# One store split into nine strided transfers, and fifteen tiny reads added, in an RMSNorm and matmul kernel

## The chip, the cores and the metric

The kernel runs on one core of one Trainium2 chip. The metric is the device time of one execution in microseconds (us). The kernel before took 210.04 us, the median of three runs (209.98 to 210.21).

## What is computed

The input x has 16,384 rows of 512 float32. Each row is divided by its root mean square and multiplied by gamma; the result goes through a matrix of 512 x 768:

```python
rms = np.sqrt(np.mean(x ** 2, axis=-1, keepdims=True) + eps)
x_norm = x / rms * gamma
return np.matmul(x_norm, weight).astype(np.float32)
```

## The kernel before

**Tiles.** The rows are worked in 128 tiles of 128 rows (`NT` = 128, `P` = 128), two tiles to a turn of the main loop (line 473, `NP` = 64 turns). A tile's row t of partition p is not row 128 t + p: sixteen tiles share a stretch of 2,048 rows in which each partition owns 16 rows that follow one another, so that a transfer moves long whole pieces per partition. The function `rows` (line 206) makes this view of x or of the output; for n tiles it gives an array of 128 partitions x n tiles x row.

**One tile.** x is loaded into `xt` (two buffers of sixteen tiles). GpSimd casts it to bf16 (`cast`, line 251); ScalarE sums the squares (`square`, line 258), and a root and a reciprocal give `rstd`. TensorE transposes pairs of bf16 as 32-bit words (line 292) and VectorE copies the transposed block out of PSUM (line 301); of some tiles VectorE does the transposition alone in blocks of 32 (lines 326 to 340). Then TensorE multiplies by the weights, which carry gamma (line 373), into one of three accumulators. ScalarE takes even tiles and VectorE odd tiles out of the accumulator, scaled by `rstd`, into `ot` (`finish_tile`, line 385).

**Transfers.** `ot` has three buffers of eight tiles, so the output goes out by eights: `o_first` and `o_size` (line 204) say which tiles make one store, and `store` (line 355) issues it when its last tile is done. The first eight tiles go as 1, 1, 2 and 4, tiles 112 to 119 as 4 and 4, the last eight as 4, 2 and 2. A new tile can be written into `ot` only when the store of 24 tiles before has landed. x comes in pieces of 2, 2, 4, 8, 8, 8, three of 16, and then pairs of 8 (line 203); `load_until` (line 247) issues them about 20 tiles ahead. All of these transfers are issued by SyncE, one after another in the order of the program, 39 in all: 22 stores, 15 loads of x and 2 of the weights. ScalarE issues one, for gamma: 2 rows of 1,024 B. So whatever is put ahead of a transfer on SyncE, a wait or an issue, holds back all those behind it.

**Order.** The class `Order` records every operation with what it reads and writes. Its method `emit` (line 37) works out the waits that are needed, gives each transfer a semaphore of its own (or one that is known to be done with) that counts to 16, and emits the streams; the middle turns of TensorE become a loop (line 152). Transfers that no later operation waits for are collected in `left` (line 163), and ScalarE waits for them at the end (line 506). The very last store (tiles 126 and 127) is issued behind everything else and is awaited last by SyncE (lines 508 to 512).

**Around the change.** The store of tiles 72 to 79 is issued in turn 39, behind the loads of tiles 96 to 111 and ahead of the store of tiles 80 to 87. The store of tiles 112 to 115 is issued in turn 57; behind it come those of 116 to 119, 120 to 123, 124 and 125, and 126 and 127, and no more loads. A store of four tiles is 128 rows of 12,288 B (1,536 KB), one for each partition.

Of the kernel before, what the change touches and what calls it, by code (L numbers as in the profile page):

```python
# [11 lines left out]
F32 = mybir.dt.float32  # L12
# [4 lines left out]
P = 128  # L17
# [149 lines left out]
def kernel(  # L167
# [9 lines left out]
    PE, DVE, ACT, POOL, SP = nc.tensor, nc.vector, nc.scalar, nc.gpsimd, nc.sync  # L177
    order = Order(tc)
# [4 lines left out]
    x = x.flatten_outer_dims()  # L183
    out = out.flatten_outer_dims()
# [3 lines left out]
    NT = N // P  # L188
    NP = NT // 2
    XG, OG = 16, 8  # L190
# [15 lines left out]
    def rows(ap, i, n):  # L206
        base, t = (x_first[i], x_size[i]) if i < XG else (i - i % XG, XG)
        return ap[base * P:(base + t) * P, :].rearrange("(p t) d -> p t d", t=t)[:, i - base:i - base + n, :]

    def sb(name, shape, dtype):  # L210
        return nc.alloc_sbuf_tensor(name, shape, dtype).ap()
# [13 lines left out]
    xTq = sb("xTq", [P, 4, 2, P, 2], BF16)  # L225
    ot = [sb(f"ot{n}", [P, OG, O], F32) for n in range(3)]
    told = sb("told", [P, 1], F32)
    ssq = sb("ssq", [P, NT], F32)
    rms = sb("rms", [P, NT], F32)
    rstd = sb("rstd", [P, NT], F32)  # L230
# [4 lines left out]
    def cells(name, slot, i, n=1):  # L235
        return [(name, slot, t) for t in range(i, i + n)]
# [118 lines left out]
    def store(i):  # L355
        first, n = o_first[i], o_size[i]
        s = first // OG % 3
        if i == first + n - 1:
            src = ot[s][:, first % OG:first % OG + n, :]
            order.transfer(SP, lambda: SP.dma_start(out=rows(out, first, n), in_=src), reads=cells("ot", s, first % OG, n))  # L360

    def hold(lhsT, cell):
        run(PE, lambda: PE.ldweights(lhsT), [cell])  # L363
# [21 lines left out]
    def finish_tile(i, engine):  # L385
        a = accumulator(i)
        s = i // OG % 3
        ends = i == o_first[i] + o_size[i] - 1 and i > o_first[i]
        before = [("told", i - 1)] if ends else []
        scale(engine, ot[s][:, i % OG, :], ops[a][:, :O], rstd[:, i:i + 1],  # L390
              [("ops", a, 0), ("ops", a, 1), ("rstd", i)] + before, [("ot", s, i % OG)])
        store(i)
        if engine is ACT and i + 1 == o_first[i] + o_size[i] - 1:
            run(ACT, lambda: ACT.mul(out=told, in_=eps_sb, mul=1.0), ["eps"], ["told", ("told", i)])  # L394
# [154 lines left out]
```

## Time and profile before

| What | Value |
|---|---|
| runs shown, median of 3 | 210.04 us |
| profiled execution, own time | 210.62 us |
| its span, first to last instruction | 208.8 us |
| granted TensorE clock, mean | 0.988 |
| TensorE busy | 194.5 us (93%) |
| VectorE, ScalarE, GpSimd busy | 149.4, 146.2, 59.8 us |
| bytes moved | 85.55 MB, HBM read 35.13, written 50.33 |
| chain that ended last, by engine | PE 71%, DMA 15%, DVE 6% |
| issue to landing, store of 8 tiles, median | 16.3 us |
| issue to landing, stores of tiles 112 to 115 and 116 to 119 | 12.0 and 9.4 us |
| issue to landing, last store, issued at 200.8 | 7.1 us |
| one store's issue on SyncE, median | 333 ns |
| one load's issue on SyncE, least, median, most | 340, 539, 823 ns |

The profile is of one execution. Its first part gives the busy time of each engine; the second cuts the span into 40 equal slices, in which a digit is the busy share in tenths. PE is TensorE's matrix multiply and PEld its weight load, DVE is VectorE, ACT ScalarE, POOL GpSimd, SP SyncE; a q behind a name means the queue of that engine, with its waits and issues. The DMA row is the mean busy share of the core's 16 DMA engines. The third part lists the DMA queues: q1 is the one that SyncE issues to, q10 ScalarE's, q8 and q14 fetch instructions. The trace behind the page has a record of each packet with its start, duration, size and queue, but not the engine that moved it.

### The profile page before, as it was taken

The page shows a single profiled execution, that of the slowest core. Times are in us where ns is not written, and L with a number is a line of the kernel's source. Part 1 is how long each engine was busy: PE and PEld are TensorE (multiplying, and loading weights), DVE is VectorE, ACT ScalarE, POOL GpSimd, SP SyncE. Part 2 cuts the span into 40 slices and gives each one's busy share as a digit, 9 for nine tenths or more (in the row PEclk, how much of TensorE's full clock was granted, in tenths as well). Part 3 has the DMA queues.
Part 4 walks back from the last instruction along what each step waited for, and adds up shares of the span by engine and source line. Part 5 has one row for each costly group of instructions (what it writes and reads, how often), then busy time and mean ns, then how long its engine had stood idle before and what let it go on. Part 6 is the DMA issues. An engine that isn't in the chain of part 4 may idle for free.

```text
span 208.8 us, 2821 instructions
## 1 busy us (share of the span) xinstructions
PE 194.5 (93%) x1236; PEld 72.7 (35%) x717; DVE 149.4 (72%) x255; ACT 146.2 (70%) x363; POOL 59.8 (29%) x34
## 2 busy tenths in 40 slices
PE   7789979999999999999999999999999999999910
PEld 1234433443344333342344333443333334433200
DVE  0455645999569975999469984999569984999410
ACT  4698888677877498774977787677877688673310
POOL 3147633009300093004900651006700265000000
PEclk9999999999999999999999999999999999999995
DMA  6999999999999999999999999999999999999991
GB/s 227 426 439 430 377 385 430 477 405 430 405 388 414 369 438 424 454 402 449 428 413 446 408 450 428 414 438 425 443 433 414 452 408 438 438 433 400 420 414 78
DMA packets 5628, 85.55 MB, mean 410 GB/s; under 512 B 626, under 2 KB 628, under 8 KB 1780
## 3 DMA queue, kind: packets, MB, share of 16 engines
q1 hardware_dynamic: 5616, 85.46, 97.4%
q8 instruction: 3, 0.05, 0.1%
q14 instruction: 5, 0.04, 0.0%
q10 hardware_dynamic: 4, 0.00, 0.0%
HBM read 35.13 MB, written 50.33 MB: 409 GB/s over the span
## 4 chain that ended last, share of the span: by engine, by line
PE 71%; DMA 15%; DVE 6%; issue 2%; SPq 1%; ACT 1%; POOL 1%; ACTq 0%
PE ps L367 62%; DMA xt<-in_x_dram 15%; PE ps L296 8%; DVE ot L350 2%; DVE xTq L340 2%; DVE xT L309 1%; POOL xb L254 1%; ACT jk L262 0%; SPq L416 0%; SPq L243 0%; ACT ot L348 0%; DVE xTq L309 0%; SPq L360 0%; DVE rstd L269 0%; SPq L544 0%
## 5 line engine op out<-in xcount | busy, mean ns | idle before, releaser
L367 PE MATMUL ps<-w_bf,xT 128*128 128x512 bf16 (+1 forms) x768 | 141.8, 326 | 1.4 <-DVE w_bf L350 0.9
L348 ACT ACTIVATE ot<-ps,rstd 128x768 f32<-128x768 f32 x64 | 57.4, 897 | 42.4 <-PE ps L367 41.2
L262 ACT ACTIVATE jk<-xt 128x512 bf16<-128x512 f32 x128 | 78.7, 618 | 6.9 <-DMA xt<-in_x_dram 6.9
L254 POOL CAST xb<-xt 128x2048 bf16<-128x2048 f32 (+3 forms) x21 | 46.2, 2218 | 114.5 <-DMA xt<-in_x_dram 95.7
L350 DVE TENSOR_SCALAR ot<-ps,rstd 128x768 f32<-128x768 f32 x64 | 64.8, 1013 | 9.0 <-PE ps L367 8.4
L363 PEld LDWEIGHTS <-xT 128*128 128x128 bf16 x384 | 37.7, 98 | 58.2 <-issue 56.9
L296 PE MATMUL ps<-ident_f,xb 128*128 128x128 f32 x200 | 54.2, 275 | 0.9 <-POOL xb L254 0.9
L340 DVE STREAM_TRANSPOSE xTq<-xq 32x256 f32<-32x256 f32 x112 | 48.8, 435 | 3.4
L367 PE MATMUL ps<-w_bf,xTq 128*128 128x512 bf16 (+1 forms) x256 | 49.0, 326 | 1.2 <-DVE xTq L309 1.2
L309 DVE COPY xT<-ps 128x1024 bf16<-128x1024 bf16 (+1 forms) x51 | 33.1, 652 | 23.1 <-PE ps L296 21.5
L296 PEld LDWEIGHTS ps<-ident_f,xb 128*128 128x128 f32 x200 | 28.4, 143 | 46.2 <-issue 42.9
L262 ACT ACTIVATION_READ_ACCUMULATOR jk<-xt 128x1 f32 x128 | 24.3, 190 | 0.0
L363 PEld LDWEIGHTS <-xTq 128*128 128x128 bf16 x128 | 12.5, 98 | 17.8 <-issue 16.1
L329 POOL CAST xq<-xt 128x2048 bf16<-128x2048 f32 x7 | 13.3, 1893 | 0.0
L269 DVE RECIPROCAL rstd<-rms 128x8 f32<-128x8 f32 (+3 forms) x20 | 3.9, 193 | 8.0 <-ACT rms L267 7.8
L267 ACT ACTIVATE rms<-ssq,eps_sb 128x8 f32<-128x8 f32 (+3 forms) x20 | 6.0, 300 | 0.6
L367 PE MATMUL ps<-warm 128*128 128x512 bf16 x10 | 4.4, 578 | 1.4 <-DVE eps_sb L425 1.4
L394 ACT ACTIVATE told<-eps_sb 128x1 f32<-128x1 f32 x20 | 3.8, 192 | 0.0
L309 DVE COPY xTq<-ps 128x1024 bf16<-128x1024 bf16 x2 | 1.4, 692 | 2.4 <-PE ps L296 2.4
L348 ACT ACTIVATE w_bf<-w_f,g_sb 128x768 bf16<-128x768 f32 x2 | 1.9, 935 | 1.5 <-DMA w_f<-in_weight_dram 0.9
L446 DVE COPY g_sb<-ps 128x4 f32<-128x4 f32 x1 | 0.2, 161 | 3.2 <-PE ps L440 3.2
L412 ACT ACT_TABLE_LOAD x1 | 1.3, 1283 | 1.5 <-SPq L503 1.5
(12 smaller groups left out, 3.6 us busy)
## 6 DMA issues: line engine op xcount, KB each, us to landing
out_dram<-ot SPq DMA_DIRECT2D x13, 3072.0 KB, 16.3
xt<-in_x_dram SPq DMA_DIRECT2D x9, 2048.0 KB, 21.0
xt<-in_x_dram SPq DMA_DIRECT2D x3, 4096.0 KB, 22.1
out_dram<-ot SPq DMA_DIRECT2D x4, 1536.0 KB, 12.0
out_dram<-ot SPq DMA_DIRECT2D x3, 768.0 KB, 8.2
w_f<-in_weight_dram SPq DMA_DIRECT2D x2, 768.0 KB, 5.7
xt<-in_x_dram SPq DMA_DIRECT2D x2, 512.0 KB, 5.2
xt<-in_x_dram SPq DMA_DIRECT2D x1, 1024.0 KB, 9.2
```

The source lines that it names most:

```text
L254: run(POOL, lambda: POOL.tensor_copy(out=xb[s][:, i % 8:i % 8 + n, :], in_=src), of, cells("xb", s, i % 8, n))
L262: run(ACT, lambda: ACT.activation(out=jk[j], in_=src[:, 0, :], func=AF.Square, accum_out=ssq[:, i:i + 1]), of, [("jk", j), ("ssq", i)])
L267: run(ACT, lambda: ACT.activation(out=rms[:, s], in_=ssq[:, s], func=AF.Sqrt, scale=1.0 / D, bias=eps_sb), [("ssq", t) for t in range(i, i ...
L269: run(DVE, lambda: DVE.reciprocal(out=rstd[:, s], in_=rms[:, s]), [("rms", i)], [("rstd", t) for t in range(i, i + n)])
L296: run(PE, lambda: PE.transpose(out=tp[b][:, t, h, :], in_=words[:, lo:lo + P], identity=ident_f), cells("xb", s, j % 4 * 2 + t) + ["ident" ...
L309: run(DVE, lambda: DVE.tensor_copy(out=dst[:, t:t + n, :], in_=src[:, t:t + n, :]), [("tp", b)], to[t:t + n])
L329: run(POOL, lambda: POOL.tensor_copy(out=xq[s], in_=src), of, [("xq", s)])
L340: run(DVE, lambda: DVE.transpose(out=dst, in_=src), [("xq", s)], ["xTq"])
L348: run(ACT, lambda: ACT.mul(out=dst, in_=src, mul=r), reads, writes)
L350: run(DVE, lambda: DVE.tensor_single_scalar(out=dst, in_=src, scalar=r, op=mybir.AluOpType.mult), reads, writes)
L363: run(PE, lambda: PE.ldweights(lhsT), [cell])
L367: run(PE, lambda: PE.add_instruction(mybir.InstMatmult(name=nc.get_next_instruction_name(), engine=mybir.EngineType.PE, ins=[PE.lower_ap(r ...
```

## The change

The store of tiles 112 to 115 (`first == NT - 16`) becomes nine transfers. Transfer `lo` takes the partitions lo, lo + 9, lo + 18 and so on: 15 partitions for lo = 0 and 1, 14 for the other seven, 128 together, with the same 12,288 B for each. Behind the store of tiles 72 to 79, SyncE issues fifteen reads of the first rows of x: read k takes k rows of 4k + 12 numbers (64 to 288 B a row, 120 rows in all) into new buffers `few` that nothing else reads or writes. The buffers take 2,640 B in each of 16 partitions.

```diff
     told = sb("told", [P, 1], F32)
+    few = {k: sb(f"few{k}", [16, 4 * k + 12], F32) for k in range(1, 16)}
     ssq = sb("ssq", [P, NT], F32)
...
         if i == first + n - 1:
             src = ot[s][:, first % OG:first % OG + n, :]
-            order.transfer(SP, lambda: SP.dma_start(out=rows(out, first, n), in_=src), reads=cells("ot", s, first % OG, n))
+            for lo in range(9) if first == NT - 16 else (None,):
+                part = slice(None) if lo is None else slice(lo, P, 9)
+                to, of = rows(out, first, n)[part], src[part]
+                order.transfer(SP, lambda to=to, of=of: SP.dma_start(out=to, in_=of), reads=cells("ot", s, first % OG, n))
+            if first == 72:
+                for k in range(1, 16):
+                    order.transfer(SP, lambda k=k: SP.dma_start(out=few[k][:k, :], in_=x[:k, :4 * k + 12]), writes=[("few", k)])
```

Each of the 23 additional transfers has a semaphore of its own and is one more that ScalarE waits for at the end. Nothing else differs.

## The prediction

> **What bounds the kernel now.** I read the page's slices first, then its queue rows, then the stretches at the end, then what SyncE waited for. All times are from the span's start. The page:
>
> ```profile
> span 208.8 us, 2821 instructions
> ...
> PE   7789979999999999999999999999999999999910
> ...
> DMA  6999999999999999999999999999999999999991
> ...
> DMA packets 5628, 85.55 MB, mean 410 GB/s; under 512 B 626, under 2 KB 628, under 8 KB 1780
> ...
> q1 hardware_dynamic: 5616, 85.46, 97.4%
> ...
> q10 hardware_dynamic: 4, 0.00, 0.0%
> ```
>
> TensorE and the transfers are both full, but TensorE stops one slice before the transfers do. Busy time by stretch (columns: length, PE, PEld, DVE, ACT, POOL with counts, granted clock, DMA share, GB/s):
>
> ```profile
> 189.00:195.00 6.00, 6.00 (x38) 1.86 (x19) 5.20 (x8) 1.89 (x3) 0.00 (x0) 1.00 1.00 425
> 195.00:201.00 6.00, 4.40 (x28) 1.17 (x12) 2.29 (x3) 1.98 (x4) 0.00 (x0) 1.00 1.00 419
> 201.00:204.00 3.00, 0.00 (x0) 0.00 (x0) 0.00 (x0) 0.00 (x0) 0.00 (x0) 0.96 0.92 381
> 204.00:208.80 4.80, 0.00 (x0) 0.00 (x0) 0.00 (x0) 0.00 (x0) 0.00 (x0) 0.50 0.17 70
> ```
>
> No compute runs after 201; from 204 the transfers are at 0.17 of 16 engines, 2.7 engines. A few late ones set the end. SyncE's own waits from 130 on say the same: the last thing awaited is a store, for 6.7 us, though the last store holds 768 KB, 1.9 us at the mean 410 GB/s.
>
> ```profile
> SPq L360 <- DVE xTq L340: 64.3, 7, 12.3
> SPq L544 <- DMA out_dram<-ot: 6.7, 1, 6.7
> ```
>
> Which engines are late is read from the packet records of the trace (start, duration, size). In full flow a packet starts 3 or 4 ns before the one ahead of it ends, so the 5616 packets of SyncE's queue fall into sixteen chains of 351: 39 transfers of 8 whole rows and a 4-byte semaphore packet each. In a chain a 12,288 B row comes every 456 ns, a 6,144 B row every 231, and a semaphore packet adds 6. At the end of the store of tiles 104 to 111, the first chain is through at 188.65; the others are later by 0.1 to 0.6 (ten), 1.3, 2.6, 3.3, 4.1 and 4.2 us. In the last store the latest chains end 3.94, 3.77, 3.30, 2.26, 1.49 and 1.01 after the first. The late ones lost their time in single stalls long before, all at once or with the instruction queues' packets (947 ns to 1.08 us at 27, 33 and 194), and never idle after. **The end is the latest chain's work:** what is added to it counts in full; what is added to the ten on-time chains has almost 4 us of cover.
>
> **The change, part by part.** The sum is made against the profiled execution: 210.62 us, 208.8 of it span. The runs shown have a median of 210.04, 0.58 lower; I add the same difference to that.
>
> *Nine transfers for one.* How a transfer of fewer rows is split is seen once: gamma's 2 rows on q10 left 4 packets, two of 1,024 B and two semaphores, so each row whole on an engine of its own. 128 rows in steps of nine make two transfers of 15 and seven of 14. With a row on each engine from the same first one on, fourteen chains get 9 rows in place of 8, one gets 2, one none. For a late chain among the fourteen: one row more, +0.456; eight semaphore packets more, 8 x 0.006 = +0.05. Bounds: rows dealt out evenly add 0; two full chains left out give -8 x 0.456 = -3.65 on those.
>
> *Which rows a chain reads.* Until now every transfer has all 128 rows, 8 to a chain; if the split is the same each time, an engine always has the same eight partitions, and a late chain disturbs nobody. With every ninth partition it reads from eight other engines' partitions or so, at a time when those engines are already in the next store. No row shows two chains at one engine's partitions. From below this costs nothing: 456 ns stays. From above, a row takes twice as long while two share: the nearest rows are packets of 24,576 B at 1,811 ns against 912 in the common stall at 57.7, and 842 against 460 for 12,288 B. What speaks for sharing is that the rate is the same for loads and stores and nearly so for all sizes (4,096 B in 155 ns, 32,768 B in 1,209: 26.4 to 27.1 GB/s), a fixed limit for each chain, on the engine or on its partitions' way out; the trace can't say which. I take the second. Ten chains of sixteen are on time. Of the late chain's nine rows, 10/16 meet a busy owner: 9 x 0.625 x 0.456 = +2.57. Before that, while it still works off the 4 us of the store before, 10/16 of the eight rows in its own partitions are fetched by on-time chains: 8 x 0.625 x 0.456 = +2.28. Both ends: 0, and all rows met, 9 x 0.456 + 8 x 0.456 = 7.75.
>
> The Trainium skill has a rule that speaks against this change: "SBUF — State Buffer", section "Door 1: The DMA port swizzle", gives each group of eight partitions one port of about 27.2 GB/s, and shows 64 partitions on eight ports at 196 GB/s against 328 for 128. Here the chains run at 26.4 to 27.1 GB/s, so two at one port would halve, as in my upper row; no run here shows it yet. By a reading in which only engines limit, the sum below would be 0.7 in place of 5.5.
>
> *Fifteen tiny reads.* 64 to 288 B a row, 120 rows in all, 7.5 a chain on average, at most 15. A packet of this size costs between the 9 ns of 4 B and the 44 ns of gamma's 1,024 B, with its semaphore 15 to 50 ns: 0 to 0.75 on one chain. I take 7.5 x 0.02 = +0.15, as the sizes are nearer the lower row. A stall as at the start, where the slowest 4,096 B took 631 ns against 159, would be 0.47 more; I keep it for the range.
>
> *SyncE's issues* cost nothing. One takes 0.33 to 0.82 us in its rows. Fifteen, 5.0 to 12.3, come behind the store at 131.7; the next is issued at 144.4 and SyncE idles 12.3 before it. Eight more, 2.7 to 6.6, come behind that at 184.9; the next is at 191.2, and the chains start these rows only at 188.6, when 4 to 11 of the nine are out. Without that cover, 116 to 119 would go out up to 0.6 late, still ahead of the late chain. The store of 88 to 95 already holds ScalarE's eviction of tile 112 for 1.19 us, and TensorE 0.4; the tiny reads add their 0.15 there. That doesn't reach the end: the last store is issued at 200.8, the latest chain starts it only at about 205.7. ScalarE's last waits (23 more, 17 to 38 ns) lie inside its wait of 5.28.
>
> *Sum* on the latest chain: 0.46 + 0.05 + 2.57 + 2.28 + 0.15 = **+5.5**: span 214.3, the profiled execution 216.1, the runs shown 215.5. Ends with this mechanism: 0.46 + 0.05 + a quarter of 7.75 = 2.4 (212.4) and 0.51 + 7.75 + 0.3 = 8.6 (218.6).
>
> **The rivals.**
> 1. *Only the ninth row counts.* The limit is the engine's own, rows don't meet: 0.46 + 0.05 + 0.15 = +0.66, 210.7. For it: in 5616 packets the pitch holds to 1 or 2 ns. Against it: that is also what fixed partitions would give.
> 2. *The late chains are the ones left out (not slower).* Fifteen- and fourteen-row transfers leave out two chains. If they are the two latest, they gain 3.65 and 2.7, and the third decides: 3.30 + 0.66 = 3.96 against 3.94, so 210.1, no change. It becomes faster only from where the third's own lag is smaller than 3.3 by more than 0.4: that lag grew by some 0.25 per big store, and if it weren't there, the fourth would decide, 2.26 + 0.66 = 2.92, -1.0, 209.0. For it: the two latest stall in the same moments (68.0, 118.3, 168.5), as if they were neighbours. Against: any two of sixteen are possible, and with sharing the third pays as well.
> 3. *The change doesn't tilt the load.* If the first engine moves on with each transfer, all get 8 or 9 rows, with 0.05 and 0.15 for packets: +0.2, 210.2. Gamma's two packets can't tell.
> 4. *Fewer engines per transfer* than rows, such as 5 for 15 and 7 for 14: 2 x 3 + 7 x 2 = 20 rows on the first five, 12 more, +5.5 without any sharing; on one engine it would be far above the range.
>
> On rivals 2 and 4: "DMA: Bandwidth & Descriptors", section "Why a DMA increments its semaphore by 16 and not by 1", has the engine count as the largest divisor up to 16 of the outer dimension, lowest-numbered engines first, so 15 and 14 here; gamma's 2 agree. Its section "Latency and other measured facts" calls engines 7 and 15 usually slower; by that only one late chain would be spared, and rival 2 gives nothing. No row here numbers the chains.
>
> **How the numbers follow.** A difference of 0.2%, 0.42 us, is about what a measurement of this kernel can tell from none. Rows that meet: 0.50 (212.4 to 218.6). Ninth row alone: 0.25 (210.2 to 211.2, the upper end with the 0.47 stall; within it 0.02 of chance lies below 0.42). Late chains left out: 0.13, of which 0.10 faster and 0.03 no change. No tilt: 0.05, no change. Fewer engines: 0.07, slower, partly above the range. Slower: 0.50 + 0.23 + 0.07 = 0.80; same: 0.02 + 0.03 + 0.05 = 0.10; faster 0.10. The likeliest is 215.5. From 210.2 to 218.6 leaves out the faster case, half of the cases of no change, and the worst of the last rival, about 0.2.
>
> **What would show it.** In the stretches: the tail after the last eviction (201 to 208.8 now) longer by 5 us, with a DMA share for one to four engines. In the packet records: the 12,288 B packets of tiles 112 to 115 and those of the stores next to them well over 460 ns, up to 900. If they stay at 460 and the end moves by 0.5 to 0.7, rival 1 holds. If the chains with no row in that store are the ones that were latest, rival 2. The tiny packets number the chains, since each chain gets another count of them. The forecast is wrong if SyncE's issues take so long that on-time chains run dry, or if the late chains of the profiled execution aren't late in the timed ones.

## The result, and the profile after

The changed kernel took 212.11 us (median of 4 runs, 211.67 to 212.57) against 210.01 before: a ratio of 1.010 (95% interval 1.0077 to 1.0124), slower by 2.1 us. The forecast was 215.5: the sign is right, the size is not, and the largest term of the sum hardly took part. The profiled execution took 212.57, its span is 210.8. Of the executions of the experiments below, two are left out of every comparison, one of e3 (215.76 us) and one of e5 (217.1), because they ran in a slower state than the others of their kernel.

The page of the changed kernel:

```profile
span 210.8 us, 2856 instructions
...
DMA  6999999999999999999999999999999999985895
GB/s 244 418 438 435 345 390 466 442 396 435 434 428 445 395 438 466 415 420 429 415 424 442 429 434 424 428 443 395 401 409 420 457 429 415 443 378 204 357 405 209
DMA packets 5980, 85.58 MB, mean 406 GB/s; under 512 B 978, under 2 KB 980, under 8 KB 2132
...
q1 hardware_dynamic: 5968, 85.49, 96.4%
```

The DMA row ends in 8, 5, 8, 9, 5: a hole of three slices where it was full before, with 204 GB/s at the bottom. Behind it the row ends in a 9 and a 5, where it had faded out before (a last slice of 1). The same two stretches in the kernel before and in the changed one (columns as before; the last three are the granted clock, the DMA share and GB/s), first before:

```profile
189.00:192.50 3.50, 3.50 (x23) 1.08 (x11) 3.33 (x6) 0.90 (x1) 0.00 (x0) 1.00 1.04 442
192.50:196.00 3.50, 3.50 (x24) 1.07 (x11) 2.12 (x3) 1.46 (x3) 0.00 (x0) 1.00 0.97 405
...
204.00:208.00 4.00, 0.00 (x0) 0.00 (x0) 0.00 (x0) 0.00 (x0) 0.00 (x0) 0.50 0.20 84
```

and after:

```profile
189.00:192.50 3.50, 3.50 (x24) 1.08 (x11) 3.31 (x6) 0.90 (x1) 0.00 (x0) 1.00 0.55 221
192.50:196.00 3.50, 3.50 (x24) 1.04 (x11) 2.48 (x3) 1.08 (x3) 0.00 (x0) 1.00 0.50 194
...
204.00:208.00 4.00, 0.00 (x0) 0.00 (x0) 0.00 (x0) 0.00 (x0) 0.00 (x0) 0.50 0.96 395
```

Half of the DMA engines' time from 189 to 196 is empty. From 204 to 208 all sixteen work, where before it was three. What emptied them is the issue, as the times show (and e2 below, without the reads). SyncE's time for the nine transfers (least, median, most, in ns) was:

```profile
L364 SPq DMA_DIRECT2D out_dram<-ot x9: 775/963/1633, 185.3 to 195.0; - x9
```

They take 10.2 us together and end at 195.77, so that the store of tiles 116 to 119 goes out at 195.81 in place of 191.19. The fifteen reads were quick to issue, 0.24 to 0.48 us each (this line's columns are the same):

```profile
L367 SPq DMA_DIRECT2D few<-in_x_dram x15: 236/296/482, 131.5 to 136.4; - x15
```

**The packet records.** The reads number the chains: a read of k rows left k packets, so the 64 B packet was seen on one chain, the 288 B packet on fifteen. By this count the five late chains are the engines 13, 12, 4, 3 and 1 (from 0), and the store of 112 to 115 gave two rows to engine 14 and none to 15, which stood idle from 187.6 to 196.9. That is the split that I had assumed. The ends of the sixteen chains tell the rest. Before, ten lie at 203.6 to 203.9, and the others at 204.6, 205.1, 205.9, 206.9, 207.40 and 207.56. After, fifteen lie between 208.10 and 208.22 and one, engine 4, at 209.24. Two things stand behind this end, 1.7 later than before:

- The hole. Fifteen chains had run empty, four of the five late ones among them, and started again together at 196.9. Their old lateness of up to 3.9 us is gone, but the time of the waiting has taken its place: 16 rows at 0.456 and 16 at 0.231 from there are 11.0 us, so 207.9, and they end at 208.1 to 208.2, 0.6 later than the latest chain before.
- The lateness of engine 4, another 1.0. It never ran empty. It was 3.9 behind the first at the end of the store of 72 to 79, and 6.2 (193.73 against 187.52) at the end of the store of 104 to 111: its first two rows behind the reads account for 1.3 of the 2.3, and most of its rows are 2 to 7% long (931 to 973 ns against 912). Then it did its nine rows in one line, from 193.73 to 198.07 (467 to 498 ns each), and began the next store 1.2 after the others, of which 1.0 is left at the end.

**What the reads did.** Their own packets took 11 to 19 ns, 0.25 us on the chain with fifteen. But behind them the first two rows of the next store (24,576 B, 912 ns each) took 2,095 and 1,444 ns on that chain, 926 and 1,711 on the one with eight reads, and 912 on those with five or fewer. That is up to 1.7 us on one chain, 1.3 of it on engine 4, a late one. So the store of tiles 88 to 95 landed later (179.07, before 178.69), and ScalarE, which needs its buffer for tile 112, sat idle for 2.0 us in place of 1.2; TensorE lost 0.7 us behind it.

### The profile page after: what moved, and what is told of

Its sections match the earlier page's. It is cut to its first block, busy times and chain, and to the rows that moved or that the text cites. A ratio compares the mean times of both kernels' runs of the same rounds, so it can differ in the third digit from the quotient of the medians.

```text
span 210.8 us, 2856 instructions
## 1 busy us (share of the span) xinstructions
PE 194.8 (92%) x1236; PEld 72.6 (34%) x717; DVE 149.3 (71%) x255; ACT 146.1 (69%) x363; POOL 59.8 (28%) x34
## 4 chain that ended last, share of the span: by engine, by line
PE 70%; DMA 15%; DVE 6%; ACT 1%; issue 1%; SPq 1%; POOL 0%; ACTq 0%
PE ps L374 62%; DMA xt<-in_x_dram 15%; PE ps L297 8%; DVE ot L351 2%; DVE xTq L341 2%; DVE xT L310 1%; ACT ot L349 1%; POOL xb L255 0%; ACT jk L263 0%; SPq L423 0%; SPq L244 0%; DVE xTq L310 0%; SPq L364 0%; DVE rstd L270 0%; SPq L551 0%
```

## The experiments

The theory after this reading (A): the loss is SyncE's issue, which runs the queues dry, with something added by the reads. The rivals: the reads alone (B), and the tilt with rows that meet at one engine's partitions, as on record (C). Each run stands beside runs of the kernel before on the same chip. A difference is that of the two medians; a ratio is the recorded estimate with its 95% interval and need not equal their quotient.

**e1, reads alone.** The two added lines of the reads, the store unchanged.

> The fifteen tiny reads alone; the store of tiles 112 to 115 is one transfer again. Theory A (SyncE's issue of the nine transfers, 0.78 to 1.63 us each in the changed kernel's trace, runs the DMA engines dry before the store of tiles 116 to 119): the reads are not what the changed kernel lost, but they cost by themselves, since nothing wipes out what they delay: in the changed kernel the chains with seven or more reads took up to 1.7 us longer for the next store, and one of the three late chains (the fifth engine by its reads) got 1.5 + 0.2 of it. If it was 3.3 late at the end before, it is now 5.0 late against 3.94 of the latest: +1.0, about 211.0. Theory B (the reads are the whole loss): +2.0, 212.0. Theory C (only the tilt and the rows that meet count): 0 to +0.2, 210.1.

Measured: 211.28 against 209.65, ratio 1.0064 (1.0043 to 1.0086), +1.6: between A and B. No hole in the DMA row (0.94 in both stretches), and the wait for the earlier store is longer. First the kernel before, then this run:

```profile
L348 ACT ACTIVATE ot<-ps,rstd x3: 900/900/900, 175.4 to 181.4; 128x768 f32<-128x768 f32 x3
...
  DMA out_dram<-ot: 1.2, 1
...
L349 ACT ACTIVATE ot<-ps,rstd x3: 900/901/902, 174.7 to 181.3; 128x768 f32<-128x768 f32 x3
...
  DMA out_dram<-ot: 1.7, 1
```

One chain ends at 208.07, 2.05 behind the next one (206.02) and 4.6 behind the first. It is engine 4 again. So the reads cost by themselves, on one late chain.

**e2, nine transfers alone.**

> The nine transfers alone, no reads. Theory A: as the changed kernel, +1.7 to +2.3, 211.7 to 212.3; SyncE's nine issues again take about 10 us, the store of 116 to 119 goes out near 195.5, and the DMA share in 189 to 196 is about one half. Theory B: 0, 210.0. Theory C (ninth row and rows that meet): +2 as well, but then with full DMA engines in 189 to 196.

Measured: 211.06 against 209.65, ratio 1.0057 (1.0038 to 1.0076), +1.4. The hole is there without any reads. No chain escapes it here, and the ends of all sixteen lie between 207.02 and 207.15:

```profile
189.00:192.50 3.50, 3.50 (x24) 1.04 (x11) 3.36 (x6) 1.30 (x2) 0.00 (x0) 1.00 0.48 184
192.50:196.00 3.50, 3.45 (x22) 1.02 (x11) 1.30 (x2) 1.59 (x4) 0.00 (x0) 1.00 0.66 270
```

B falls; A's size (+1.7 to +2.3) was 0.3 to 0.9 too high. The ten runs form two groups, three at 210.2 to 210.4 and seven at 210.9 to 211.7; the profile is of the lower one, so what makes the upper one was not seen.

**e3, the same tilt in two issues.**

```diff
-            order.transfer(SP, lambda: SP.dma_start(out=rows(out, first, n), in_=src), ...)
+            for part in (slice(0, 126), slice(126, P)) if first == NT - 16 else (slice(None),):
+                to, of = rows(out, first, n)[part], src[part]
+                order.transfer(SP, lambda to=to, of=of: SP.dma_start(out=to, in_=of), ...)
```

> The store of tiles 112 to 115 as two transfers, of partitions 0 to 125 and of 126 and 127. If a transfer uses the largest number of engines up to 16 that divides its rows, 126 rows are 9 on each of fourteen engines, partition 9e + i on engine e as its row i: the same rows on the same engines in the same order as the nine transfers, in two issues. Theory A: the DMA engines don't run dry, and what is left is the ninth row, some meeting rows, and late chains that stay late: +0.5 to +1, 210.5 to 211.0, with the DMA share in 189 to 196 at 0.95 or more. Theory C: the same loss as with nine, +2 or more (my forecast on record would be +5.5 less the reads), 212 to 215.

Measured: 212.96 (five executions, 212.50 to 214.54) against 209.65, ratio 1.0127 (1.0092 to 1.0162), +3.3. This is theory C, against what A expected. The DMA engines are busy and move little (0.93 and 0.95, but 330 GB/s where 0.97 gave 405 before):

```profile
189.00:192.50 3.50, 3.50 (x24) 1.08 (x11) 3.34 (x6) 1.10 (x2) 0.00 (x0) 1.00 0.93 330
192.50:196.00 3.50, 3.45 (x23) 1.08 (x11) 1.47 (x3) 1.78 (x4) 0.00 (x0) 1.00 0.95 331
```

I take a busy share at a low rate for the mark of rows that wait for one another: 47 of the 384 rows of 12,288 B behind 180 took over 600 ns, 20.5 us in excess of 460 together; before there were 2, in the changed kernel 7 (2.9 us). Chains end between 203.0 and 211.5. So fewer issues make it worse, not better: what the nine issues lose in empty queues, they save in long rows.

**e4, eight transfers of every eighth partition** (`slice(lo, P, 8)`, 16 rows each).

> The store of tiles 112 to 115 as eight transfers of every eighth partition: 16 rows each, one on each of sixteen engines, no tilt, no reads. It tells whether SyncE's issue is slow for every transfer of few rows or only for those that don't fill sixteen engines. Theory A with a slow issue for 14 and 15 alone: eight issues of 0.33 to 0.5, 3 to 4 us, hidden; 210.0 to 210.3 unless rows meet. Theory A with a slow issue for any strided transfer: eight of 0.8 to 1.6, up to 11 us, +1 to +2. Theory C: every eighth partition puts engines in pairs on the same eight partitions, all rows of this store take up to twice their 460 ns, 3.65 more on every chain: up to +3.7, 213.7.

Measured: 212.82 against 209.65, ratio 1.012 (1.0081 to 1.016), +3.2. The issues took 0.57 to 2.4 us, so it isn't the odd count of 14 or 15 that makes them slow. Of the first 128 rows, half took over 772 ns, a quarter over 927: twice 460.

**e5, the nine transfers in mid-run** (`first == 40`).

> The nine transfers moved to the store of tiles 40 to 47 (rows of 24,576 B), in the middle of the run, where the queues hold 10 us of transfers or more and the next store is 12.6 us away; no reads. Theory A1 (SyncE's issue of a transfer of few large rows is slow by itself, 0.77 us and more): the issues take 0.8 to 1.6 us here too, but nothing runs dry. Theory A2 (the issue is slow because the queues have something in hand): 1.4 us and more for all nine. With nothing dry, late chains stay late and rows meet, as in the two-issue form: theory C gives +3 to +8 for rows twice as long (213 to 218), theory A alone only the ninth row of 0.9, +1.0, 210.7.

Measured: 212.60 (three executions, 212.27 to 215.18) against 209.71, ratio 1.0173 (1.0095 to 1.0251), +2.9: just below what C gave (+3 to +8), and well above the +1.0 of A alone. With full queues the issue is steady, 0.77 for 14 rows and 0.80 to 0.99 for 15 (A1):

```profile
L363 SPq DMA_DIRECT2D out_dram<-ot x9: 765/769/994, 83.8 to 90.5; - x9
```

Its profiled execution took 217.1, far above the other three, so nothing but SyncE's issues is read from it.

**e6, the reads spread, five behind each of three stores.**

```diff
-            if first == 72:
-                for k in range(1, 16):
+            if first in (72, 80, 88):
+                for k in range(1 + (first - 72) // 8, 16, 3):
```

> The same fifteen reads, but five behind each of the stores of tiles 72, 80 and 88 (1, 4, 7, 10, 13; 2, 5, ...; 3, 6, ...), so that no chain has more than five in a row; store of 112 as one transfer. Theory R1 (a chain with seven or more small packets in a row can't read ahead, and its next large rows wait: nothing at up to five reads, up to 1.7 us at fifteen): the cost is the packets' own 0.02 each, +0.1 to +0.3, 209.8 to 210.0 where the run before is 209.65. Theory R2 (each small read costs 0.1 us or so of waiting, however many follow one another): +1.6 as in one block, 211.3.

Measured: 210.16 against 209.71, ratio 1.0019 (1.0002 to 1.0036), +0.45, of which R1 had expected 0.1 to 0.3 and R2 1.6. The same reads, not in one row, cost a quarter. ScalarE doesn't wait for a store at tile 112 at all.

**e7, nine transfers of neighbouring partitions.**

```diff
+            cuts = [0, 15, *range(30, P + 1, 14)] if first == NT - 16 else [0, P]
+            for lo, hi in zip(cuts, cuts[1:]):
+                part = slice(lo, hi)
```

> The store of tiles 112 to 115 as nine transfers of neighbouring partitions (15, 15 and seven of 14), no reads: the same numbers of rows, engines and issues as the nine strided ones, but within a transfer up to four engines read the same eight partitions. If the step of nine makes SyncE's issue slow, it is 0.3 to 0.5 us here and the queues don't run dry; if few large rows do, 0.8 to 1.6 again, and the store of 116 goes out near 195. Theory C: packets of 1 to 2 us in numbers (over 80 above 600 ns), +4 or more, 214; theory A alone: as the strided nine, +1.4, 211.1.

Measured: 212.38 against 209.71, ratio 1.0126 (1.0075 to 1.0178), +2.7, between what A alone (+1.4) and C (+4) gave. The issues are as slow (0.41 for the first, then 0.76 to 1.83), so the step of nine is not the reason. Of the first 128 rows a quarter took over 1,142 ns, the longest 2,182.

**e8, a load in three transfers** (tiles 48 to 63 as 112, 12 and 4 partitions), a try at a faster version.

> A try at a faster version: the load of tiles 48 to 63 (rows of 32,768 B) in three transfers of 112, 12 and 4 rows. If they go to 16, 12 and 4 engines, the last four engines (two of them the latest chains, by the reads' count) get one row of 1.21 us less, the first four one more, the others as before. No reads, no nine. Without meeting rows the latest chain is then the one that is 3.30 late, in place of 3.94: -0.6, 209.0 where the run before is 209.65. With meeting rows, since 7 rows an engine shift the partitions: the late chains lose 1 to 4 us in this load, +0.5 to +3, 210.2 to 212.7.

Measured: 220.66 against 209.71, ratio 1.0531 (1.0487 to 1.0575), +11. 124 rows of 32,768 B took over 1.6 us (24 before), 267 GB/s at a share of 1.01 in 60 to 72, and then TensorE had nothing to do for almost ten us:

```profile
60.00:72.00 12.00, 11.89 (x79) 4.70 (x47) 11.33 (x21) 7.58 (x18) 0.00 (x0) 1.00 1.01 267
72.00:84.00 12.00, 2.43 (x17) 0.68 (x7) 2.98 (x6) 2.19 (x6) 2.15 (x1) 0.69 0.97 317
```

I read it as what e3 had shown, with larger rows: engines that are dealt other partitions than in the transfers beside it. The records have neither engine nor partition, so that this is not shown.

**e9, the two-issue form of e3 behind an empty queue,** and **e10, the empty queue alone.** Both hold the store of 112 to 115 back until tile 119 is done; e10 has `slice(None)` in place of the two parts.

```diff
+            if first == NT - 16:
+                return
+            if first == NT - 12:
+                for part in (slice(0, 126), slice(126, P)):
+                    to, of = rows(out, NT - 16, 4)[part], ot[s][:, :4, :][part]
+                    order.transfer(SP, lambda to=to, of=of: SP.dma_start(out=to, in_=of), reads=cells("ot", s, 0, OG))
```

> The two-issue form of e3 (126 and 2 partitions, the same rows on the same engines as the nine transfers), but issued only when tile 119 is done, at 191.2, just ahead of the store of 116 to 119; the queues then run empty from about 187.5 on the chains that are on time, and the late ones have caught up to within 1 us when the 126 rows start at 192.3. No reads. Theory C1 (rows meet only where chains are out of step, and an empty queue puts them in step): few long rows (under 10 above 600 ns, where e3 had 47); the end is the start at 192.3 + 9 rows (4.2) + the 24 later rows (11.0) + the landing: 207.9 + 0.5 to 1 for the latest chain, +0.3 to +1.2, 210.0 to 210.9 where the run before is 209.7. Theory C2 (the 126-row form costs by its partitions, in step or not): as e3, +3.8, or more by the 4 us of empty queue, 213.5 to 217.

Measured: 213.81 against 209.58, ratio 1.0201 (1.017 to 1.0232), +4.2. C1 falls. The chains did start in step (191.4 to 191.8), but 37 rows took over 600 ns. The rate stays low once the chains run:

```profile
192.50:196.00 3.50, 3.45 (x22) 1.07 (x11) 1.49 (x3) 1.79 (x4) 0.00 (x0) 1.00 1.02 337
```

So the long rows come even then. As I read it, engines 14 and 15 have no rows and go straight on to the next store, into partitions that the others are still reading.

> The same delay of the store of tiles 112 to 115 until tile 119 is done, as one transfer of 128 partitions. All theories that make the late chains' work the end: the on-time chains stand idle for 4 to 5 us, the late ones for 1 us at most, and all start again at 192.3 with 32 rows (14.7 us): the latest end at 207.0 to 208.0, -0.3 to +0.5, 209.4 to 210.2. If idle time on the on-time chains counts in full, +4, 213.7.

Measured: 211.38 against 209.58, ratio 1.0095 (1.0056 to 1.0135), +1.8, against an expected -0.3 to +0.5. One plain transfer, no tilt, 3 long rows, and a loss of the same size, with nothing added but a hole:

```profile
189.00:192.50 3.50, 3.50 (x23) 1.06 (x11) 3.34 (x6) 0.90 (x1) 0.00 (x0) 1.00 0.37 154
192.50:196.00 3.50, 3.45 (x23) 1.00 (x12) 1.91 (x3) 1.67 (x3) 0.00 (x0) 1.00 0.94 387
```

Fifteen chains end between 206.73 and 206.91, one at 208.59. That one lost its time in rows of 846, 655 and 841 ns around an instruction packet of 16,384 B at 195.3 (954 ns). Such a packet came in the kernel before too (947 ns at 194.1), but on a chain that had cover. With all chains in step nobody has any. So most of this loss is that chain's, and not the hole's own length. The latest chain before ended at 207.56 in an execution that took 1.0 more than the median beside e10; by that I estimate 206.5 here, and the fifteen are only 0.2 to 0.4 later. What the other four executions lost was not seen.

**e11, the change again,** on the chip of e9 and e10.

> The changed kernel once more on the chip of these two, to have it beside them. +1.6 to +2.6. SyncE's nine issues sum to 9 to 11 us, the waits at tile 112 again hold ScalarE for 1.5 to 2.5 us, fewer than 12 rows of 12,288 B above 600 ns.

Measured: 211.43 against 209.58, ratio 1.009 (1.0061 to 1.012), +1.85. The issues sum to 9.9 us, 7 rows are long. One expectation failed: ScalarE did not wait for a store at tile 112; its waits there are for TensorE, 0.9 at most. The chains end between 207.42 and 207.84, and one at 208.07, so no chain is far behind the others, and the hole sets the end.

## Why the prediction was wrong, point by point

**The late chains set the end: right** for the kernel before, and the change did away with it. I had taken their lateness for a fixed sum to which things are added. It is lost in a gap that is long enough for them to catch up, and what then counts is when the chains start again. Only a chain that is later than the gap is long keeps lateness: engine 4 in the profiled execution of the change, none in e2.

**"SyncE's issues cost nothing": this is the step that failed.** I took 0.33 to 0.82 us from rows of 128 partitions, and let 4 to 11 of the nine be out by 188.6. It was 0.78 to 1.63, so that three were out by then and the last left at 195.77. That the forecast is wrong if on-time chains run dry was on record; it happened. By e2 the nine issues alone are worth +1.4. The end follows the restart: on the chains that ran empty the store of 116 to 119 starts at 195.8 to 195.9 in e2, at 196.2 to 196.7 in e11 and at 196.9 to 197.0 in the changed kernel, and they end 11.2 to 11.4 later in all three. e10's +1.8 shows the other price of a hole, the lost cover, which the changed kernel did not pay in its profiled execution: its instruction packet came at 192.9, inside the hole, and not on engine 4. **The ninth row** (0.46) is there: engine 4, which had no hole, took 4.34 us for its nine, 0.48 each. On the other chains it lies in the hole.

**Rows that meet, +4.85: such long rows exist, the changed kernel hardly had them.** That was the largest term, and it is the second one that was mis-sized: with the issues this slow, its condition (full queues) wasn't there. e3 has, by the split assumed there, the same rows on the same engines without the hole, and lost 3.3, where my sum without the reads was 5.4; its long rows reached 1,735 ns. (The 842 ns that I had taken for the nearest row stands right behind an instruction packet in the kernel before, as the 841 in e10 does; it was no example of two rows that meet.) In the changed kernel there were 7 such rows (2.9 us in excess), and none of them on the chain that ended last: as I read it, chains with one row in hand at a time and a pause behind it rarely meet. Engine 4's nine rows took 467 to 498 ns each. My 10/16 assumed queues that never pause. The Trainium skill's rule ("SBUF — State Buffer", section "Door 1: The DMA port swizzle", one port for each group of eight partitions) agrees with the sizes: by its map, e4 puts two engines on a port and a quarter of its rows took over 927 ns; e7 puts up to four there, and rows reached 2,182.

**Tiny reads, +0.15: mis-sized.** The packets' own cost was right (0.02 each). The stall behind them, for which I kept 0.47, was up to 1.7, and 1.3 on engine 4, where it counts as the sum counts what is added to a late chain. e6 shows that it comes from the reads' standing in one row: with five in a row at most, the same fifteen cost +0.45, in one block +1.6 (e1). With both parts the losses don't add up, 1.6 and 1.4 make 2.1 or 1.85. My reading is that the end is the later of the two, and that the hole swallows the lateness of a chain up to its own length. The wait at tile 112 is another trace of the reads: the gap between the issue of the store of 104 to 111 and the first of the nine is 7.16 us, where e2 has 6.35, and that moves the hole. It doesn't come every time: in e11 the gap is 6.34.

**Split of the rows: right,** as far as counts of rows show it. Rival 3 (no tilt) and rival 4 (fewer engines) fall by the packet counts. Rival 2 falls too: the engines left out, 14 and 15, were on time. Rival 1 (+0.66) falls by e3.

**What stays open.** Why SyncE takes 0.77 us for 14 large rows when it takes 0.33 for 128 and 0.37 for 14 small ones, and why single issues take up to 2.4 when the queues are nearly empty; e4 and e7 only rule out the odd count and the step. The count of rows isn't all of it: behind the eight transfers of e4, plain stores of 128 rows took 0.84, 0.90 and 1.41 to issue, where they take 0.33 in the kernel before. Where rows meet isn't settled either: a row's partition and its addresses in HBM go together in all of these runs, so that no run tells the partitions' side from the memory's. Why engine 4's rows are longer than the others', and what parts e2's runs into two groups, wasn't seen. No version beat the kernel before.

## What to carry to other kernels

Before a transfer is cut into pieces, look up how long the issuing queue takes for such a piece, and compare their sum with what the DMA engines still have in hand; a row for another shape is no bound. A transfer that doesn't take all 128 partitions can give a row to another engine than its neighbours in the queue do, and in e3, e8 and e9 some rows then took up to 3.8 times as long: look for a full DMA share at a low rate. If the late engines set the end, a gap that hits the others isn't free: it takes away the cover under which later stalls were hidden.

## What the runs showed of the hardware that I had not expected

- SyncE's issue of a transfer to HBM took 0.33 us for 128 rows of 12,288 B, 0.40 for 126, mostly 0.76 and more for 14, 0.57 and more for 16, and up to 2.4 near empty queues.
- A row of fifteen small reads (30 packets with their semaphores, 0.25 us) kept a DMA engine from going on at its rate for another 1.7 us; five did not.
- One load of 4 MB cut into transfers of 112, 12 and 4 partitions (e8) cost 11 us, more than any wait in this study.
